# The first chunk of a four-layer hybrid network on one core: squares in four parts, weights in row buffers, two engines in written order

## The chip, the cores and the metric

One core of a Trainium2 chip runs the whole program in a single launch. The metric is the device time of one execution in microseconds (us). The program is a stack of four layers over 1040 tokens (16 learned tokens ahead of 1024), all in fp32, where each fp32 product is made of three products of "high" and "low" fp32r parts.

## What is computed

The reference, cut to what the change touches: the norm ahead of the first layer and that layer's projections. The other layers (a gated recurrence, a second recurrence, and attention again) follow in the same way.

```python
def rmsnorm(x, g):
    y = x * lax.rsqrt(jnp.mean(x * x, axis=-1, keepdims=True) + EPS)
    return y * g

def attention_branch(u, w_in, q_gain, k_gain, sinks, w_out, valid, pos):
    q, k, v, z = _split(u @ w_in, (A_W, A_KVW, A_KVW, A_W))
    q = rope(rmsnorm(q, q_gain), pos)
    k = rope(rmsnorm(k, k_gain), pos)
    o = sliding_window_attention(q, k, v, sinks, valid)
    return (o * silu(z)) @ w_out

for i in range(4):
    u = rmsnorm(h, norm_gain[i])
    h = h + branch[i % 3](u, ...)
```

## The kernel before

The residual `x` lies in SBUF as 8 tiles of 128 features by 1040 tokens. Tokens are worked in three chunks of 400, 384 and 256 (`CHUNKS`); a chunk's normalized input is kept as a high part `uh` and a low part `ul`, 8 tiles each, and the first 16 tokens again in `um`, 16 columns of high and 16 of low for each tile, so that the block of 16 tokens is one narrow operand.

The work is a list of steps, each with a cost, a function and perhaps a `pre` that loads and splits weights. TensorE (PE) runs in the order in which the steps are called. VectorE (DVE), ScalarE (ACT), GpSimd (POOL) and SyncE's transfers (SP) are ordered by the framework's scheduler from its own estimate of when each instruction can start. A `pre` is called ahead of its step by up to `LOOKAHEAD`.

The norm of a chunk: ACT squares the 8 tiles (`sq`, L369), DVE adds them (L373), PE multiplies the sum with a matrix of ones (`stat`, L381) so that each partition has the sum over all features, ACT makes the reciprocal root by Ln and Exp (`rstd_from`, L353 and L354), and then, for each tile, DVE multiplies x, gain and root (L407) and `split` copies the result rounded to fp32r on ACT (L187) and subtracts it on DVE (L188). For the first chunk POOL then copies 16 columns of either part to `um` (L412). Squares come in `PARTS` = 2 groups of four tiles, each with its own product with ones.

Weights come from HBM in halves of 512 columns: a transfer into one of two `raw` buffers (L232), then the same `split`. A key tile's first half holds feature tiles 0 to 3. The value weights are two pieces, `src0` with feature tiles 0 to 3 and `src1` with 4 to 7, in halves of two feature tiles.

The start: the 8 transfers of the first chunk of x, the norm's steps for chunk 0 (`norm.stats`, `norm.unit`), then the first layer's head. For chunk 0 that is `kv`: two of four parts of the key projection (feature tiles 0 to 3, L254), the value projection with the first four feature tiles for the four token blocks (L295 for the 16 tokens, L299 for three blocks of 128), the key's other two parts, and the value blocks' second halves. Into this the squares and products with ones of chunks 1 and 2 are put at shares `FIRST` of the head's cost. Then come chunk 1's key tile (a product of 384 columns), and so on.

## Time and profile before

| | |
|---|---|
| median of 3 runs | 2611.88 us |
| lowest and highest | 2609.99 and 2614.97 us |
| the profiled execution | 2610.83 us |
| its span, first to last instruction | 2609.0 us |
| mean granted TensorE clock | 0.995 |

Busy time is that of one engine summed over its instructions. PE's matmuls are pipelined, and their ends are modelled, so the distance from one start to the next says more than a duration does. An idle time stands in brackets behind an instruction with what ended it. "Granted clock" is the share of full speed that TensorE was allowed: 1.00 is 2.4 GHz and 0.50 is 1.2 GHz.

### The profile page before, as it was taken

What the parts mean: (1) busy time and instruction counts of PE and PEld (TensorE: products, weight loads), DVE (VectorE), ACT (ScalarE), POOL (GpSimd) and SP (SyncE); (2) the same over time, 40 slices, a digit from 0 to 9 for tenths busy, and PEclk for the clock granted to TensorE, in tenths of its full rate; (3) what the DMA queues carried; (4) which work ended last, traced back from release to release, by engine and by line L of the source; (5) the groups of instructions that cost most, each with busy time, mean ns of one, the idle gap of its engine ahead of it and who ended that gap; (6) DMA issues with size and microseconds to landing.
All of it is one profiled execution on the core that took longest, in us unless ns stands there. A gap on an engine that the chain in (4) does not pass through costs nothing.

```text
span 2609.0 us, 56062 instructions
## 1 busy us (share of the span) xinstructions
PE 2558.0 (98%) x21048; PEld 2459.0 (94%) x21048; DVE 1980.3 (76%) x5487; ACT 1725.9 (66%) x4757; POOL 154.1 (6%) x538
## 2 busy tenths in 40 slices
PE   7999999999999999999999999999999999999999
PEld 6899889899999999999999999999999999999999
DVE  6677777986767676767677788978787978677776
ACT  6777776566464646464646857878585867768872
POOL 1100100000000000000000000201001011000000
PEclk9999999999999999999999999999999999999999
DMA  4111111021111111111110101011110111111112
GB/s 136 56 43 50 46 37 47 17 67 58 41 58 41 58 41 58 41 58 41 55 61 34 57 27 42 30 38 34 34 42 26 42 62 45 54 44 47 53 38 82
DMA packets 74048, 126.81 MB, mean 49 GB/s; under 512 B 11552, under 2 KB 25760, under 8 KB 73776
## 3 DMA queue, kind: packets, MB, share of 16 engines
q1 hardware_dynamic: 73776, 123.23, 14.5%
q8 instruction: 165, 2.70, 0.4%
q14 instruction: 107, 0.88, 0.1%
HBM read 108.34 MB, written 4.26 MB: 43 GB/s over the span
## 4 chain that ended last, share of the span: by engine, by line
PE 81%; DVE 10%; ACT 6%; issue 1%; DMA 1%; POOL 0%; SPq 0%; DVEq 0%; ACTq 0%; POOLq 0%
PE pj L254 39%; PE pj L337 16%; PE pj L299 11%; PE po L682 2%; PE pt L660 1%; PE pm L614 1%; PE pm L615 1%; DVE t L407 1%; PE pa L534 1%; DVE ul L188 1%; PE po L918 1%; PE pj L295 1%; PE pm L890 1%; DVE X L1153 1%; DVE X L1155 1%
## 5 line engine op out<-in xcount | busy, mean ns | idle before, releaser
L254 PE MATMUL pj<-uh,wh 128*128 128x384 f32 (+2 forms) x2592 | 870.9, 336 | 3.7 <-ACT uh L187 3.6
L254 PE MATMUL pj<-ul,wh 128*128 128x384 f32 (+2 forms) x2592 | 835.3, 322 | 2.9 <-DVE ul L188 2.8
L254 PE MATMUL pj<-uh,wl 128*128 128x384 f32 (+2 forms) x2592 | 832.9, 321 | 0.1
L254 PEld LDWEIGHTS pj<-uh,wh 128*128 128x128 f32 x2592 | 491.3, 190 | 24.1 <-issue 12.7
L254 PEld LDWEIGHTS pj<-ul,wh 128*128 128x128 f32 x2592 | 491.2, 190 | 8.7 <-DVE ul L188 5.5
L254 PEld LDWEIGHTS pj<-uh,wl 128*128 128x128 f32 x2592 | 490.9, 189 | 0.5 <-DVE wl L188 0.4
L188 DVE TENSOR_TENSOR wl<-wr,wh 128x512 fp32r<-128x512 f32 x336 | 227.9, 687 | 58.1 <-ACT wh L187 55.4
L340 DVE TENSOR_TENSOR x<-x,pj 128x384 f32<-128x384 f32 (+2 forms) x480 | 235.4, 510 | 43.2 <-PE pj L337 41.3
L187 ACT CAST wh<-wr 128x512 fp32r<-128x512 f32 x337 | 203.3, 616 | 83.0 <-PE pj L337 26.8
L299 PE MATMUL pj<-wh,uh 128*128 128x256 f32 x896 | 258.1, 288 | 0.0
L337 PE MATMUL pj<-yh,wh 128*128 128x384 f32 (+2 forms) x768 | 253.0, 329 | 0.0
L299 PE MATMUL pj<-wh,ul 128*128 128x256 f32 x896 | 252.4, 282 | 0.0
L299 PE MATMUL pj<-wl,uh 128*128 128x256 f32 x896 | 252.3, 282 | 0.0
L337 PE MATMUL pj<-yl,wh 128*128 128x384 f32 (+2 forms) x768 | 247.4, 322 | 3.1 <-DVE yl L188 3.1
L337 PE MATMUL pj<-yh,wl 128*128 128x384 f32 (+2 forms) x768 | 246.8, 321 | 0.0
L299 PEld LDWEIGHTS pj<-wh,uh 128*128 128x128 f32 x896 | 169.3, 189 | 1.1 <-issue 0.3
L187 ACT CAST yh<-r 128x400 fp32r<-128x400 f32 (+2 forms) x144 | 68.6, 477 | 153.2 <-PE pj L337 141.7
L299 PEld LDWEIGHTS pj<-wl,uh 128*128 128x128 f32 x896 | 169.3, 189 | 0.5
L299 PEld LDWEIGHTS pj<-wh,ul 128*128 128x128 f32 x896 | 169.3, 189 | 0.0
L428 ACT ACTIVATE t<-t 128x384 f32<-128x384 f32 (+2 forms) x240 | 117.8, 491 | 76.5 <-DVE t L427 74.8
L427 DVE SCALAR_TENSOR_TENSOR t<-pj,t 128x384 f32<-128x384 f32 (+2 forms) x192 | 98.8, 514 | 78.2 <-ACT t L426 75.3
L337 PEld LDWEIGHTS pj<-yl,wh 128*128 128x128 f32 x768 | 144.9, 189 | 5.0 <-DVE yl L188 4.7
(265 smaller groups left out, 5431.4 us busy)
## 6 DMA issues: line engine op xcount, KB each, us to landing
wr<-in_b_win SPq DMA_DIRECT2D x128, 256.0 KB, 2.6
wr<-in_a_win SPq DMA_DIRECT2D x80, 256.0 KB, 2.7
wr<-in_c_win SPq DMA_DIRECT2D x64, 256.0 KB, 2.7
r<-rowsd SPq DMA_DIRECT2D x16, 520.0 KB, 5.4
wr<-in_a_wout SPq DMA_DIRECT2D x32, 256.0 KB, 2.7
wr<-in_b_wout SPq DMA_DIRECT2D x32, 256.0 KB, 2.6
t<-t SPq DMA_DIRECT2D x96, 48.0 KB, 1.9
wr<-in_c_wout SPq DMA_DIRECT2D x16, 256.0 KB, 2.7
```

The source lines that it names most:

```text
L187: s.copy(h, src)
L188: v.tensor_tensor(l, src, h.bitcast(F32), op=ALU.subtract)
L254: pe.matmul(acc[:, :cn], a[:, k, :], b[:, k, c0 : c0 + cn], start=(k == 0 and i == 0), stop=(k == KT - 1 and i == 2))
L295: pe.matmul(acc[:48, :256], um[:, k, :], m[:, kk, :], start=(k == 0 and m is wh), stop=(k == KT - 1 and m is wl))
L299: pe.matmul(acc[:cn, :256], a[:, k, c0 : c0 + cn], m[:, kk, :], start=(k == 0 and i == 0), stop=(k == KT - 1 and i == 2))
L337: pe.matmul(acc[:, :cn], a[:, k, mc], b, start=(k == 0 and i == 0), stop=(k == 1 and i == 2))
L340: v.tensor_tensor(x[:, m, c0 : c0 + cn], x[:, m, c0 : c0 + cn], acc[:, :cn], op=ALU.add)
L407: v.scalar_tensor_tensor(u, x[:, k, cs], ngain[:, self.i, k : k + 1], self.acc[n], op0=ALU.mult, op1=ALU.mult)
L427: v.scalar_tensor_tensor(a[:, :cn], z, 0.0, a[:, :cn], op0=ALU.min, op1=ALU.subtract)
L428: s.activation(a[:, :cn], a[:, :cn], AF.Exp)
L534: pe.matmul(st[:, 2 * k : 2 * k + 2], sq[:, z : z + P], R["masks"][:, 0:P:64], start=True, stop=True)
L682: pe.matmul(po[64 * hh : 64 * hh + 64, q0 - c0 : q0 - c0 + nq], V[kb][:kn, vc : vc + 64], ws[hh]["Pt"][:kn, u, ki, :nq], start=(ki == 0), ...
```

## The change

It concerns the first chunk of the first layer, and the order of what is loaded at the start.

- The first chunk's squares are taken in four parts of 4, 2, 1 and 1 tiles, so that four products with ones run in place of two. Chunks 1 and 2 keep two parts of four.
- The first key tile's weights and both pieces of the first value weights are loaded into three of the nine row buffers, straight behind x and the gains. Their splits are cut into halves (`late`) and placed by hand.
- From the first square to the last weight half of this stage, DVE and ACT run in program order. The written order is: the squares; the key's first half; Ln and Exp; then tiles 0 to 7, in which a tile's low part comes after the next tile's high part, with the key's second half behind tile 0, the value halves behind tiles 2, 3, 5 and 7.
- PE gets 12 products of zeros (`um`, 384 columns) ahead of the first product with ones, and 16 products of 128 columns behind the last.
- The 16-token copies become two for either half of the tiles, one on ACT and one on DVE, and no POOL copies. The memset of `um` moves from POOL to DVE.
- The value block of 16 tokens is multiplied after the three blocks of 128, in either half.
- The first layer's masks and columns are loaded ahead of the second chunk of x; the scaling of the columns and the two rope loads move to the end of the ordered stretch. `ident` is loaded later. Chunk 1's squares move to shares 0.4 to 0.95 of the head's cost from 0.3 to 0.9.

```diff
-PARTS = 2, 2, 2
-FIRST = 0.3, 0.9, 0.3, 0.7
+WARM = 12, 16
+FIRST = 0.4, 0.95, 0.3, 0.7
...
-    g.memset(um.bitcast(F32), 0.0)
+    v.memset(um.bitcast(F32), 0.0)
...
+    def load_row(src):
+        raw = row()
+        for z in (slice(0, 512), slice(512, 1024)):
+            sp.dma_start(raw[:, z], src[:, z])
+        return raw
+
     load_x(0)
-    sp.dma_start(ident, ins["ident"])
     sp.dma_start(ngain, ins["ngain"])
+    early = [load_row(ins["a_win"][0][k]) for k in (0, 2, 3)]
+
+    def warm(b, n):
+        def fn():
+            pe.matmul(psa()[:, : b.shape[-1]], rones, b, start=True, stop=True)
+
+        return [[0.0, fn, None] for _ in range(n)]
...
         for z in (slice(0, 512), slice(512, 1024)):
+            if row is not None:
+                late.append(lambda z=z: split(row[:, z], h[:, z], l[:, z]))
+                continue
...
+        def halves(self, n):
+
+            c0, cn = CHUNKS[n]
+            cs = slice(c0, c0 + cn)
+            u = {}
+
+            def high(k):
+                def fn():
+                    u[k] = tmp()[:, :cn]
+                    v.scalar_tensor_tensor(u[k], x[:, k, cs], ngain[:, self.i, k : k + 1], self.acc[n],
+                                           op0=ALU.mult, op1=ALU.mult)
+                    s.copy(uh[:, k, cs], u[k])
+
+                return [0.0, fn, None]
+
+            def low(k):
+                def fn():
+                    v.tensor_tensor(ul[:, k, cs], u[k], uh[:, k, cs].bitcast(F32), op=ALU.subtract)
+                    if k % 4 == 3:
+                        ks = slice(k - 3, k + 1)
+                        s.copy(um[:, ks, :NMETA], uh[:, ks, :NMETA].bitcast(F32))
+                        v.tensor_copy(um[:, ks, 32 : 32 + NMETA], ul[:, ks, :NMETA].bitcast(F32))
+
+                return [0.0, fn, None]
+
+            return [high(0)] + [z for k in range(1, KT) for z in (high(k), low(k - 1))] + [low(KT - 1)]
...
-            kv = kg0[0][:2] + vg[0][::2] + kg0[0][2:] + vg[0][1::2]
+            kp, vp = kg0[0], vg[0]
+
+            def take(step):
+                pre, step[2] = step[2], None
+
+                def first_half():
+                    pre()
+                    late.pop(0)()
+
+                return [0.0, first_half, None], [0.0, lambda: late.pop(0)(), None]
+
+            ordered = tc.manual_schedule(engines={mybir.EngineType.DVE, mybir.EngineType.Activation})
+            begin, end = [0.0, ordered.__enter__, None], [0.0, lambda: ordered.__exit__(None, None, None), None]
+            wk, wv0, wv1 = take(kp[0]), take(vp[0]), take(vp[1])
+            s0, u0 = first.stats(0, (4, 2, 1, 1)), first.halves(0)
+            kv = [begin] + warm(um.rearrange("p k c -> p (k c)"), WARM[0]) + s0[:-1] + [wk[0]] + s0[-1:]
+            kv += warm(rones, WARM[1]) + u0[:3] + [wk[1]] + u0[3:7] + [wv0[0]] + u0[7:9] + kp[:2]
+            kv += [wv0[1]] + u0[9:13] + [wv1[0]] + u0[13:] + [wv1[1], end]
+            kv += [vp[2], vp[4], vp[6], vp[0]] + kp[2:] + [vp[3], vp[5], vp[7], vp[1]]
...
-        head[0].insert(0, [0.0, enter, None])
+        if first:
+            enter()
+        else:
+            head[0].insert(0, [0.0, enter, None])
+        head[0].insert(head[0].index(end) if first else 1, [0.0, rope_load, None])
...
-    steps += norm.stats(0, PARTS[0]) + [norm.unit(0, k) for k in range(KT)]
...
-                st = norm.stats(n, PARTS[n])
+                st = norm.stats(n, (4, 4))
...
+    sp.dma_start(ident, ins["ident"])
     load_x(1)
```

## Rows read from the trace of the kernel before

**Rows 1.** Page, busy time of the engines over the span.

```profile
PE 2558.0 (98%) x21048; PEld 2459.0 (94%) x21048; DVE 1980.3 (76%) x5487; ACT 1725.9 (66%) x4757; POOL 154.1 (6%) x538
```

**Rows 2.** Stretches: us, busy per engine, granted clock, DMA share, GB/s.

```profile
5.00:10.00 5.00, 1.67 (x2) 0.50 (x2) 2.75 (x5) 3.62 (x7) 0.00 (x0) 1.00 0.99 324
...
0.00:50.00 50.00, 35.26 (x194) 29.39 (x195) 34.43 (x70) 33.37 (x70) 12.88 (x27) 0.97 0.52 165
...
100.00:150.00 50.00, 47.78 (x369) 43.10 (x370) 36.93 (x108) 39.15 (x133) 4.31 (x16) 1.00 0.14 40
...
900.00:950.00 50.00, 50.00 (x319) 49.83 (x318) 35.64 (x75) 25.72 (x58) 0.00 (x0) 1.00 0.13 43
```

**Rows 3.** Timeline (start, us, engine, line, operation, idle before): sums of squares.

```profile
6.51 2.68 ACT L369 ACTIVATE t<-x 128x400 f32<-128x400 f32 x5 [0.80 <-DMA x<-in_xT]
...
7.80 1.67 PE L381 MATMUL pa<-t,ones 128*128 128x400 f32 x2 [7.80 <-DVE t L373]
8.19 1.94 DVE L373 TENSOR_TENSOR t<-t,t 128x400 f32<-128x400 f32 x3 [0.54 <-ACT t L369]
...
10.18 1.70 PE L381 MATMUL pa<-t,ones 128*128 128x400 f32 x2 [0.71 <-DVE t L373]
...
11.92 0.59 ACT L353 ACTIVATE t<-pa,eps 128x400 f32<-128x400 f32 x1 [1.79 <-PE pa L381]
12.41 0.61 ACT L187 CAST wh<-wr 128x512 fp32r<-128x512 f32 x1
12.92 0.54 ACT L354 ACTIVATE t<-t 128x400 f32<-128x400 f32 x1
13.05 0.69 DVE L188 TENSOR_TENSOR wl<-wr,wh 128x512 fp32r<-128x512 f32 x1 [2.19 <-ACT wh L187]
13.66 1.72 DVE L407 SCALAR_TENSOR_TENSOR t<-x,ngain,t 128x400 f32<-128x400 f32 x3
```

**Rows 4.** Timeline: the normalized tiles of the first chunk.

```profile
14.32 1.61 ACT L187 CAST uh<-t 128x400 fp32r<-128x400 f32 x3 [0.87 <-DVE t L407]
...
15.30 1.54 DVE L188 TENSOR_TENSOR ul<-t,uh 128x400 fp32r<-128x400 f32 x3
...
18.88 1.28 DVE L188 TENSOR_TENSOR wl<-wr,wh 128x512 fp32r<-128x512 f32 x2
...
24.06 0.68 DVE L188 TENSOR_TENSOR wl<-wr,wh 128x512 fp32r<-128x512 f32 x1
```

**Rows 5.** Timeline, TensorE: products of the first chunk.

```profile
22.34 0.45 PE L295 MATMUL pj<-wh,um 128*48 128x256 f32 x1 [1.15 <-POOL um L412]
...
26.01 0.28 PE L299 MATMUL pj<-wh,ul 128*128 128x256 f32 x1
26.13 0.28 PE L299 MATMUL pj<-wh,uh 128*128 128x256 f32 x1
```

**Rows 6.** Stretches of half a us around the clock's fall and rise.

```profile
22.00:22.50 0.50, 0.16 (x1) 0.17 (x2) 0.46 (x2) 0.44 (x2) 0.50 (x3) 0.55 0.70 195
...
25.00:25.50 0.50, 0.50 (x4) 0.50 (x4) 0.40 (x2) 0.50 (x2) 0.26 (x1) 0.53 0.91 320
```

**Rows 7.** Timeline: end of the first chunk and the second chunk's norm.

```profile
32.04 0.81 PE L381 MATMUL pa<-t,ones 128*128 128x384 f32 x2
...
32.88 0.58 ACT L353 ACTIVATE t<-pa,eps 128x384 f32<-128x384 f32 x1 [0.21 <-PE pa L381]
...
34.05 1.68 DVE L407 SCALAR_TENSOR_TENSOR t<-x,ngain,t 128x384 f32<-128x384 f32 x3 [0.94 <-ACT t L354]
...
36.95 0.34 PE L254 MATMUL pj<-uh,wh 128*128 128x384 f32 x1
...
41.11 0.58 DVE L550 TENSOR_TENSOR r<-r,r 128x400 f32<-128x400 f32 x1
...
42.21 0.44 PE L254 MATMUL pj<-ul,wh 128*128 128x384 f32 x1 [0.44 <-DVE ul L188]
```

**Rows 8.** Timeline, SyncE: issue of the second chunk of x.

```profile
7.00 3.86 SPq L172 DMA_DIRECT2D x<-in_xT  x8
```

More of the change, by code (lines that the diff above doesn't have):

```diff
@@ L222, in gate_rows_proj, with weights @@
         return groups
-    def weights(src, kind, inrow=False):
+    late = []
+    def weights(src, kind, inrow=False, row=None):
         if inrow:
@@ L235, in weights, with proj @@
         return h.rearrange("p (k c) -> p k c", k=k), l.rearrange("p (k c) -> p k c", k=k)
-    def proj(src, evac, chunks=CHUNKS):
+    def proj(src, evac, chunks=CHUNKS, row=None):
         st = {}
         def pre():
-            st["w"] = weights(src, "m")
+            st["w"] = weights(src, "m", row=row)
         groups = []
@@ L269, in put_v, with proj_v @@
             s.copy(V[:cn, :256], acc[:cn, :256])
-    def proj_v(src0, src1, evac):
+    def proj_v(src0, src1, evac, rows=(None, None)):
         st = {}
         def pre0():
-            st[0] = weights(src0, "v")
+            st[0] = weights(src0, "v", row=rows[0])
         def pre1():
-            st[1] = weights(src1, "v")
+            st[1] = weights(src1, "v", row=rows[1])
         groups = []
@@ L365, in __init__, with sq @@
             self.i, self.acc, self.ps = i, {}, {}
-        def sq(self, m, n, c0, cn, size=KT):
+        def sq(self, m, n, c0, cn, new=None):
             q = tmp()[:, :cn]
             s.activation(q, x[:, m, c0 : c0 + cn], AF.Square)
-            if m % size == 0:
+            if m == 0 if new is None else new:
                 self.acc[n] = q
@@ L385, in stat, with stats @@
             return [4 * cn * MM, fn, None]
-        def stats(self, n, parts):
+        def stats(self, n, sizes):
             c0, cn = CHUNKS[n]
-            size = KT // parts
             def squares(part):
                 def fn():
-                    for m in range(part * size, (part + 1) * size):
-                        self.sq(m, n, c0, cn, size)
+                    m0 = sum(sizes[:part])
+                    for m in range(m0, m0 + sizes[part]):
+                        self.sq(m, n, c0, cn, m == m0)
                 return [0.0, fn, None]
-            return [z for k in range(parts) for z in (squares(k), self.stat(n, k, parts))]
+            return [z for k in range(len(sizes)) for z in (squares(k), self.stat(n, k, len(sizes)))]
+        def halves(self, n):
[18 more added lines that the diff above has]
+            return [high(0)] + [z for k in range(1, KT) for z in (high(k), low(k - 1))] + [low(KT - 1)]
         def unit(self, n, k):
@@ L450, in enter, with rope_load @@
             sp.dma_start(cons, ins["a_cols"][j])
+        def rope_load():
+            cons = R["cons"]
             v.tensor_scalar(cons[:, 0:1], cons[:, 0:1], 0.125, None, op0=ALU.mult)
@@ L512, in work_rows, with qk_proj @@
             return work
-        def qk_proj(src, gcol, work, fsplit, ch, scales=None):
+        def qk_proj(src, gcol, work, fsplit, ch, scales=None, row=None):
             late = {}
@@ L558, in finish @@
                         (D_Q[2], fsplit(lambda: late[n][0], n, c0, cn))]
-            return proj(src, evac, ch), [finish(n, *c) for n, c in enumerate(ch)]
+            return proj(src, evac, ch, row), [finish(n, *c) for n, c in enumerate(ch)]
         def tile_of(groups, events):
@@ L712, in layer_a @@
                           fin if t == 7 else None, t == 5) for t in (1, 3, 5, 7)}
-        kg0, kfin0 = qk_proj(win[0], 1, work_rows(3), k_split(0), CHUNKS)
+        kg0, kfin0 = qk_proj(win[0], 1, work_rows(3), k_split(0), CHUNKS, row=early[0] if first else None)
         kg1, kfin1 = qk_proj(win[1], 1, work_rows(1), k_split(1), CHUNKS)
-        vg = proj_v(win[2], win[3], v_evac)
+        vg = proj_v(win[2], win[3], v_evac, early[1:] if first else (None, None))
         qg = {t: qk_proj(win[4 + t], 0, tmps, q_split(t), chunks, t) for t in range(8)}
@@ L1342, in hybrid_kernel @@
         if i % 3 == 0:
-            head, body, oa, ob = layer_a(i, i // 3, tail is None, i == 3, fin)
+            head, body, oa, ob = layer_a(i, i // 3, norm if tail is None else None, i == 3, fin)
         elif i % 3 == 1:
@@ L1373, in hybrid_kernel @@
     ahead, k = 0.0, 0
-    while steps[k][2] is None:
-        k += 1
-    steps[k][2]()
-    steps[k][2] = None
+    sp.dma_start(ident, ins["ident"])
     load_x(1)
-    k = 0
     for n, (cost, fn, pre) in enumerate(steps):
```

## The prediction

> **What bounds the kernel now.** I read the busy times first, then stretches of 50 us, then the timeline of the first 45 us engine by engine, and last the granted clock in half-microsecond steps. TensorE is busy for 2558 of 2609 us [rows 1], and a stretch from the middle has no hole in it [rows 2]: there a change off TensorE gives nothing. Of the first 50 us TensorE is busy for 35.3 [rows 2], so 14.7 us are empty, and nearly all of them lie before 22.3. The change works on that hole alone.
>
> The hole goes like this. ScalarE's last square ends at 9.19 (6.51 + 2.68), VectorE's last addition at 10.13, and the second product with ones runs from 10.18 to the start of Ln at 11.92. Ln to the first normalizing instruction (call its start t, here 13.66) takes 1.74 us, since a weight cast at 12.41 stands ahead of Exp and a weight subtraction at 13.05 ahead of t [rows 3]. The second chunk has the same pair with nothing between: 32.88 to 34.05, 1.17 us [rows 7]. From t on VectorE is the limit: eight pairs of normalize and subtract, 0.57 and 0.51 us each, and four weight subtractions of 0.64, done by 24.74, which is t + 11.1 [rows 3, 4]. TensorE waits tile by tile, last 1.15 us for a GpSimd copy at 22.34; from there it runs without a break [rows 5] to the second chunk's first key product at 36.95, t + 23.3 [rows 7]. Two further gates follow: the second chunk's product with ones at 32.04, t + 18.4, and the tile that TensorE waits for at 42.21 [rows 7].
>
> **The change part by part.**
>
> *Squares in four parts.* The end no longer needs the last addition: 10.13 becomes 9.19, 0.94 us. But four products with ones replace two. One lasts 1.70 us at half clock [rows 3] and 0.81 at full [rows 7]; about 0.15 of either is drain and up to 0.2 is the first load, so in a chain each costs some 1.33 or 0.67 us. The second part's sum is there at about 8.75, since tiles 4 and 5 are squared by 8.13 and added in 0.58. All at full clock: 8.75 + 3 x 0.67 + 0.15 = 10.9 for Ln. All at half: 7.80 + 4 x 1.33 + 0.2 = 13.3. Two of each: 7.80 + 2.67 + 1.33 + 0.15 = 11.95 if the clock rises midway, 12.3 if it falls midway. Ln at 11.92 is what we have, so this part alone is worth between +1.0 and -1.4 us, near zero in the middle: TensorE has become the chain there, and the clock decides.
>
> *Weight halves around Ln and Exp.* The key's first half is cast right behind the last square (9.2 to 9.8 if landed by then), well before Ln, and the second half waits until behind tile 0. So 1.74 becomes 1.17: t = 12.1, 13.1 to 13.5, or 14.5. I take 13.3, a gain of 0.36.
>
> *Program order.* What comes behind t is longer. VectorE now has five weight halves there, not four, and each costs more than its 0.62: ScalarE casts it only after the tile's own cast, VectorE stands at the subtraction meanwhile, and ScalarE's next tile cast stands behind that. Walked through in units of rows 4 (normalize 0.57, hand-over to ScalarE 0.65 from start to start, tile cast 0.53, weight cast 0.61, subtract 0.50): key half 2 ends at t + 3.0, tile 3's low part at t + 7.5, the first value piece at t + 6.4 and 9.1, tile 7 at t + 14.2, the last weight half at t + 15.2. Of these 15.2 us, 12 are work and 3.3 are five waits of 0.6 to 0.8. Before, all this was over at t + 11.1. Queued behind each wait are the next tile's normalize and, for TensorE, its three products.
>
> *TensorE behind t.* The blocks of 128 tokens go first, so TensorE last waits at t + 9.1, for the value half with tiles 2 and 3. The GpSimd copies are gone and nothing of the 16 tokens is late: two pairs of copies of 64 columns, each under a 400-column cast (0.53 us) and at least nothing, stand on ScalarE and VectorE; I take 0.2 each, in the walk. What is left then is 66 products of 256 columns at 0.12, 16 narrow ones at 0.12, 12 of 400 columns at 0.18 and two products with ones at 0.65: 7.8 + 1.9 + 2.2 + 1.3 = 13.2 us, to t + 22.3 at full clock. Tile 7 (t + 14.2) and the last weight half (t + 15.2) are first used at t + 14.6 and t + 15.7, just in time. Now the clock: it stood at half from 22.0 to 25.4, after a stretch in which TensorE had waited tile by tile [rows 5, 6], and this cost 1.7 us. The new stretch up to t + 9.1 is as thin. With the same fall: t + 23.8. Before: t + 23.3.
>
> *Second chunk.* Its squares lie behind the ordered stretch: ScalarE is free at t + 14.5, eight squares take about 4 us, the last addition ends near t + 19.3; if the scheduler slips some into the waits, earlier. TensorE reaches the product at t + 18 (full) or t + 19.5 (half). So that gate comes at t + 18 to 19.5, against t + 18.4: +0.4 to -1.1.
>
> *What is hidden.* The 12 products of zeros (0.18 us each at full, twice that at half) end before the first product with ones at 7.80; if they didn't, the excess would be paid. The 16 small ones take 0.9 to 1.8 us of the 1.8 between the last product with ones and the first tile cast. The `um` memset stands on VectorE before any square is there. On SyncE's queue the second chunk of x, issued from 7.00 before [rows 8], now stands behind four more weight halves, the masks and the columns: some 1.3 MB, about 4 us at the 324 GB/s of 5 to 10 us [rows 2]; it then lands near 18 to 19, and its squares start at t + 14.5 = 27.8. Without that cover each us late would count. The third chunk and the rope rows move likewise; rope is read first at 41.11 [rows 7]. Whether casting from a row buffer costs other than from `raw` no row shows; the same shape on the same engine took 0.61 us [rows 3], and 0.1 us either way for six is the bound.
>
> *Sum.* Gain 0.36 at t; behind t, -0.5 at half clock or +1.0 at full, and by the second chunk -1.1 to +0.4: I take -0.1. Together 0.3 us off the profiled execution's 2610.83. On the median, 1.05 us higher, that is 2611.6. The corners are t = 12.1 with full clock, 2.2 us faster, and t = 14.5 with half, 2.0 us slower.
>
> One rule speaks for a better end. The Trainium skill (TensorE: Matmul & The Clock Gate, "What's actually happening") says that sustained work lifts the clock and that it falls back after an idle window. The trace has it falling at 22.05 although TensorE's last wait had been 1.15 us and it had done products shortly before [rows 5, 6]; by the row a thin stretch is enough. So I don't count on the zeros holding until 7.80.
>
> **The rivals.**
> 1. *Full clock throughout.* The zeros lift the clock and it stays: t = 12.1 and t + 22.3. Gain 2.1 us: 2609.8. For it: the skill's rule above. Against: some two us without a product between the zeros (begun at about 1.3, 4 us at half clock) and 7.80, and the fall at 22.05.
> 2. *The written order doesn't hold VectorE.* If weight casts slip ahead of tile casts, the 3.3 us of waits go and TensorE's last wait is near t + 6.5: 2.6 us more, 2609.0, with rival 1 as well 2607.2. Against: the order is written, cast behind cast.
> 3. *Slower: half clock through the four products.* t = 14.5, end t + 23.8, the second chunk's squares late: 2613.6. It decides if the clock is at half at 7.80 and doesn't rise before the fourth product; the two products before were at half (1.70 us).
> 4. *The rest is ordered anew.* Everything later is ordered by the scheduler from estimates that now start elsewhere. From 100 to 150 TensorE stands idle for 2.2 us [rows 2], and each fall of the clock costs 1.7. Two or three such pieces either way: 2607 or 2616.
>
> **How the numbers follow.** No change to speak of 0.54, rival 1 0.14, rival 2 0.10, rival 3 0.12, rival 4 0.10 (0.06 for faster). About 0.2%, 5.2 us, is what a measurement of this kernel can tell from no change. The corners of the sum lie within it; beyond it on the fast side are half of rival 2 and most of rival 4's fast half, and a tail of rival 1, 0.13; on the slow side rival 4's slow half and a tail of rival 3, 0.07; the rest is 0.80. The range holds all but the outer parts of rival 4 and of rival 2, with the scatter of the runs of before (2610.0 to 2615.0): 2606.5 to 2615.0.
>
> **What the new profile would show.** Right: Ln between 11 and 13 with no weight cast between it and Exp; VectorE idle 0.6 to 0.8 us ahead of each weight subtraction behind t, released by ScalarE; no GpSimd copy; last low part at about t + 14; the first 384-column key product between 34.5 and 38. Wrong if: the four products with ones follow at 0.67 us (rival 1); VectorE has no such waits (rival 2); Ln comes after 13 (rival 3); or the start gains and loses as told, and the time still moves by over 3 us, in stretches behind 50 (rival 4).

## The result: 0.23% slower

| | before | after |
|---|---|---|
| median of 10 runs each, side by side | 2610.55 us | 2617.07 us |
| lowest and highest | 2607.12 and 2614.97 | 2611.86 and 2620.13 |
| ratio, with 95% interval | | 1.0023 (1.0014 to 1.0033) |
| the profiled execution, and its span | 2610.83 and 2609.0 us | 2620.13 and 2618.3 us |
| mean granted clock of that execution | 0.995 | 0.993 |

The time lies 5.5 us above the forecast and 2.1 us above the upper end of its range. The profiled execution is the slowest of the ten, so 3 us of its 9.3 us are scatter. Another profile of the changed kernel (run e5 below) spans 2615.2 us, and another of the kernel before (e6) 2608.3.

Busy times (the page) and stretches of the changed kernel (as [rows 1] and [rows 2]):

```profile
PE 2569.9 (98%) x21080; PEld 2469.2 (94%) x21080; DVE 1979.7 (76%) x5488; ACT 1725.4 (66%) x4759; POOL 143.5 (5%) x521
```

```profile
0.00:50.00 50.00, 41.03 (x204) 34.11 (x204) 31.67 (x67) 31.04 (x66) 2.32 (x10) 0.93 0.50 164
50.00:100.00 50.00, 45.68 (x315) 41.94 (x315) 34.20 (x90) 38.28 (x110) 2.05 (x9) 0.97 0.20 61
100.00:150.00 50.00, 47.78 (x356) 43.18 (x355) 34.83 (x100) 36.37 (x123) 5.09 (x17) 0.97 0.14 40
900.00:950.00 50.00, 50.00 (x306) 50.00 (x305) 33.17 (x68) 29.74 (x69) 0.00 (x0) 1.00 0.13 43
```

TensorE is 5.8 us busier in the first 50 us. Its added products more than account for that: the zeros take 4.18 us, and four products with ones take 5.67 where two took 3.37. VectorE does 2.8 us less there: it falls behind.

The timeline of the changed kernel up to t, the first normalizing instruction (as [rows 3]; start, us, engine, line, operation, count, idle before; each fp32 product counts as two instructions):

```profile
1.45 4.18 PE L186 MATMUL pa<-um,ones 128*128 128x384 f32 x12 [1.45 <-DVE um L167]
7.51 5.67 PE L398 MATMUL pa<-t,ones 128*128 128x400 f32 x8 [1.88 <-DVE t L390]
...
5.53 3.27 ACT L386 ACTIVATE t<-x 128x400 f32<-128x400 f32 x6 [1.39 <-DMA x<-in_xT]
8.93 0.62 ACT L199 CAST wh<-r 128x512 fp32r<-128x512 f32 x1
13.22 0.59 ACT L370 ACTIVATE t<-pa,eps 128x400 f32<-128x400 f32 x1 [3.67 <-PE pa L398]
13.84 0.54 ACT L371 ACTIVATE t<-t 128x400 f32<-128x400 f32 x1
...
14.41 1.18 DVE L427 SCALAR_TENSOR_TENSOR t<-x,ngain,t 128x400 f32<-128x400 f32 x2 [4.14 <-PE pa L186]
```

The last square ends at 8.80, earlier than the 9.19 of before, but Ln waits until 13.22 for four products that stand back to back from 7.51: 5.67 us, 1.4 each.

VectorE and TensorE from t on (as [rows 4, 5, 7]):

```profile
16.70 0.69 DVE L200 TENSOR_TENSOR wl<-r,wh 128x512 fp32r<-128x512 f32 x1 [0.49 <-ACT wh L199]
...
20.08 0.69 DVE L200 TENSOR_TENSOR wl<-r,wh 128x512 fp32r<-128x512 f32 x1 [0.62 <-ACT wh L199]
...
22.58 0.69 DVE L200 TENSOR_TENSOR wl<-r,wh 128x512 fp32r<-128x512 f32 x1 [0.54 <-ACT wh L199]
...
25.96 0.69 DVE L200 TENSOR_TENSOR wl<-r,wh 128x512 fp32r<-128x512 f32 x1 [0.62 <-ACT wh L199]
...
28.07 0.57 DVE L435 TENSOR_TENSOR ul<-t,uh 128x400 fp32r<-128x400 f32 x1
28.55 0.55 DVE L390 TENSOR_TENSOR t<-t,t 128x384 f32<-128x384 f32 x1
29.02 0.19 DVE L439 CAST um<-ul 128x64 fp32r<-128x64 f32 x1
29.12 0.69 DVE L200 TENSOR_TENSOR wl<-r,wh 128x512 fp32r<-128x512 f32 x1
...
29.86 2.35 DVE L390 TENSOR_TENSOR t<-t,t 128x384 f32<-128x384 f32 x4
```

```profile
21.86 0.70 PE L271 MATMUL pj<-ul,wh 128*128 128x400 f32 x1 [1.53 <-DVE ul L435]
...
30.56 0.88 PE L398 MATMUL pa<-t,ones 128*128 128x384 f32 x2 [0.49 <-DVE t L390]
...
34.90 0.81 PE L398 MATMUL pa<-t,ones 128*128 128x384 f32 x2
...
39.32 0.33 PE L271 MATMUL pj<-uh,wh 128*128 128x384 f32 x1
```

The written order's waits are there, and tile 7's low part comes at 28.07, t + 13.66. The last addition to the second chunk's first sum of squares starts at 29.86, behind that part and the last weight half. At 30.56 TensorE stands for VectorE at the *first* of the second chunk's two products with ones, which reads this sum; 8.76 us of its work lie between that product and the second chunk's first key product.

One table for all profiles, the experiments' too, in us from t, but for t itself. "Ln" is counted from the end of the last square; "low 7" is tile 7's low part; "ones 1, 2" are the second chunk's products with ones; "key" is its first key product.

```
                           t      Ln   low 7  ones 1  ones 2   key
before                   13.66   2.73   9.91   14.60   18.38   23.29
before, again (e6)       12.86   2.67   9.90   13.47   17.34   22.25
after                    14.41   4.42  13.66   16.15   20.49   24.91
after, again (e5)        13.21   2.97  13.66   16.15   20.49   24.91
e1  no products          14.08   4.14  13.66   16.07   20.43   24.84
e3  two parts            12.85   2.71  13.67   16.16   21.91   25.15
e4  own order            13.87   2.84  10.26   13.31   19.19   23.61
e7  22 of zeros          12.36   1.90  13.66   16.15   20.49   24.91
e8  e1 + e3 + e4         13.33   2.72   9.67   12.62   18.40   21.64
e9  first ones later     13.27   3.40  13.66   17.14   20.05   24.57
e10 no small products    14.23   4.28  13.66   16.15   20.47   24.89
e11 22, none, later      11.95   1.86  13.66   17.97   20.88   25.41
e12 e8, shares of before 13.20   2.70   9.67   12.63   19.51   23.93
e13 before, four parts   14.19   4.32   9.17   14.88   18.66   23.56
e14 e11, own order       12.33   1.93  10.28   15.44   17.51   21.93
e16 e8, first later      13.54   2.71   9.68   12.90   14.97   19.38
e17 e16, written order   12.82   2.70  13.66   16.79   19.70   24.23
e18 e16 again            13.30   2.70   9.68   13.05   15.11   19.53
e2  before, 32 small     12.98   2.54   9.90   13.20   16.98   21.89
e15 before, 38 small     13.89   3.17   9.84   14.74   18.52   23.42
```

### The profile page after: what moved, and what is told of

The parts are those of the page before. It is cut to its first block, busy times and chain, and to the rows that moved or that the text cites. A ratio compares the mean times of both kernels' runs of the same rounds, so it can differ in the third digit from the quotient of the medians.

```text
span 2618.3 us, 56111 instructions
## 1 busy us (share of the span) xinstructions
PE 2569.9 (98%) x21080; PEld 2469.2 (94%) x21080; DVE 1979.7 (76%) x5488; ACT 1725.4 (66%) x4759; POOL 143.5 (5%) x521
## 3 DMA queue, kind: packets, MB, share of 16 engines
q8 instruction: 166, 2.72, 0.4%
## 4 chain that ended last, share of the span: by engine, by line
PE 80%; DVE 11%; ACT 6%; issue 2%; DMA 1%; SPq 0%; POOL 0%; DVEq 0%; ACTq 0%; POOLq 0%
PE pj L271 38%; PE pj L354 16%; PE pj L316 11%; PE po L729 2%; PE pt L707 1%; PE pm L661 1%; PE pa L581 1%; PE pm L662 1%; DVE t L451 1%; DVE ul L200 1%; PE po L987 1%; PE pm L959 1%; ACT Sm L686 1%; PE pj L312 1%; DVE wl L200 1%
```

## The experiments

Each run's time is a median of 11, and its ratio, with a 95% interval, is to 21 to 33 runs of the kernel before, timed beside it. The intervals are some 0.0009 wide to either side, 2.3 us, so two runs that differ by less than about 3 us are not told apart by their times alone. Diffs are against the changed kernel unless another is named.

**The two kernels once more.** e5 is the changed kernel, e6 the kernel before (a profile and a single time, 2610.1 us).

> The changed kernel itself, profiled and timed once more, to tell what of its first trace is the change and what is that one execution. Theory E (the loss is in the first chunk and carried, the rest is where each execution's half-clock stretches happen to fall): first 384-column key product again 1.5 to 4 us later than the 34.9 to 37.0 of the kernel before, but the difference between 75 and 300 us does not repeat: other stretches at half clock than 95.5 and 116 us. Theory A (weight halves land late at fixed places): the same two late landings near 91 and 218 us. Time 2615 to 2618 us either way.

> The kernel before itself, profiled once more. Theory E: its first 384-column key product moves between 34.5 and 37.5 us with the place of the half-clock stretch, and the stretches behind 50 us fall elsewhere than 80, 261 and 517 us. Theory A: the same places. One time, 2605 to 2616 us.

e5: 2616.51 us, 1.0023 (1.0014 to 1.0032). The loss is there again, and so are the two late weight halves: 4.6 us after issue at 85.24 and 4.2 after issue at 211.53.

**e1, no products of zeros and no small ones; e7, more of zeros.**

```diff
-WARM = 12, 16
+WARM = 0, 0      # e1;  e7: 22, 16
```

> The changed kernel without its 28 products of zeros and ones ahead. Theory A (the start costs 2.4 to 2.8 us, by TensorE's half clock through four products with ones and by VectorE's waits; the rest of the loss comes later in layer one, because 64 more TensorE instructions shift the points at which TensorE's next block of instructions is fetched, and the fetch then shares a transfer engine with a weight half that is needed at once): t (first normalizing instruction) stays near 14.4, since the four products were at half clock with the zeros too; the later loss of 3 to 4 us goes; 2613 to 2614 us against 2610.6 for the kernel before and 2617 for the changed one. Rival B (the zeros help the start and the loss is all in the start or its order): t later by 0.5 us or more, total 2617 to 2618.

> The changed kernel with 22 products of zeros in place of 12, so that TensorE is not idle for two us before the first product with ones at 7.5. Theory E: with 12 the clock is back at half by then or during the four products (they ran 0.67 us per load in the changed kernel, half clock); with 22 it is up from about 6 us and stays, the four products take 0.7 us each or less, Ln at 11 to 11.5 instead of 13.2, t at 12.2 to 12.7 instead of 14.4, the first 384-column key product 1.5 to 2 us earlier: 2615. Rival F (zeros do nothing for the clock): t at 14 or later, 2617 or more.

e1: 2614.9 us, 1.0018 (1.0009 to 1.0026). e7: 2613.92 us, 1.0019 (1.0010 to 1.0028). Without any such products t is 14.08 and Ln comes 4.14 us behind the last square. The five traces with 12 of zeros and four parts have 2.84 to 4.42 there, so the 12 helped in some executions and not in others. With 22 they reach up to the products with ones:

```profile
1.45 6.20 PE L186 MATMUL pa<-um,ones 128*128 128x384 f32 x22 [1.45 <-DVE um L167]
7.50 0.83 PE L398 MATMUL pa<-t,ones 128*128 128x400 f32 x2
8.84 2.28 PE L398 MATMUL pa<-t,ones 128*128 128x400 f32 x6 [0.51 <-DVE t L390]
```

The clock is up (0.83 us a product), Ln comes 1.90 us behind the last square and t at 12.36. That is the prediction's full-clock rival, and yet the second chunk's key product stands at t + 24.91 as in the changed kernel: from t to there the clock isn't what binds.

**e3, two parts; e13, four parts in the kernel before.**

```diff
-            s0, u0 = first.stats(0, (4, 2, 1, 1)), first.halves(0)
+            s0, u0 = first.stats(0, (4, 4)), first.halves(0)
```

```diff
# e13, against the kernel before, with stats() and sq() taking sizes as in the changed kernel
-PARTS = 2, 2, 2
+PARTS = (4, 2, 1, 1), (4, 4), (4, 4)
```

> The changed kernel with the first chunk's squares in two parts of four again. Theory A: the last addition ends near 9.5 and one product with ones of 1.7 us at half clock follows, Ln at 11.3 instead of 13.2, t at 12.5 instead of 14.4, first 384-column key product 1.5 to 2 us earlier than 39.3; the loss behind 50 us stays: 2615 to 2615.5. Rival C (four parts are no burden): t not before 14, 2617.

> The kernel before with one part of the change: the first chunk's squares summed in four parts (4, 2, 1, 1). Theory A (the products with ones follow at 0.67 us, as in the changed kernel, and the four are the chain): Ln comes 1 to 1.3 us later against the last square than in the kernel before (there 2.7 us behind its end), t moves by that, and the time is 2611 to 2612, not to be told from the kernel before. Rival (the prediction's step: one addition less on the chain): Ln comes up to 1 us earlier against the last square and the time is 2609.5 to 2610.5.

e3: 2614.02 us, 1.0014 (1.0005 to 1.0023). e13: 2611.71 us, 1.0005 (0.9996 to 1.0014). The four parts alone, in the kernel before (TensorE, then ScalarE):

```profile
7.29 5.67 PE L381 MATMUL pa<-t,ones 128*128 128x400 f32 x8 [7.29 <-DVE t L373]
...
13.00 0.59 ACT L353 ACTIVATE t<-pa,eps 128x400 f32<-128x400 f32 x1 [2.14 <-PE pa L381]
```

The column "Ln" of the table gives their price: 2.7 us behind the last square with two parts; with four, 4.1 to 4.4 where all of it runs at half clock, 2.8 to 3.4 where the clock changes midway, 1.9 at full clock. Theory A of e13 holds for Ln. The total of e13 doesn't show it. In e3, against its expectation, a second loss is gone as well, far behind the start (see e10 below), so its time doesn't price the four parts.

**e4, VectorE and ScalarE in the scheduler's order; e8, that with two parts and no products.**

```diff
-            ordered = tc.manual_schedule(engines={mybir.EngineType.DVE, mybir.EngineType.Activation})
+            ordered = ExitStack()
```

> The changed kernel with VectorE and ScalarE ordered by the scheduler as before, the steps called in the same sequence. Theory A: weight casts are put into ScalarE's idle time, VectorE's waits of 0.6 us ahead of weight subtractions go in part, the last low part ends 1 to 3 us earlier than 28.6 after t; TensorE's first 384-column key product 0 to 2 us earlier than 39.3: 2615 to 2617. Rival D (the written order is no burden): tile 7 and the key product as in the changed kernel or later, 2617 or more.

> The changed kernel with squares in two parts of four, VectorE and ScalarE in the scheduler's order, and no products ahead: what stays are the row buffers for weights, the 16-token copies in two, the blocks of 128 first and the order of loads. Theory E (the loss lies in four parts at half clock and in the written order): t at 12 to 13, the first 384-column key product at 35 to 37, time 2609.5 to 2611.5, no slower than the kernel before. Rival G (the loss lies in what stays, as the second chunk of x landing later): 2613 or more.

e4: 2613.52 us, 1.0012 (1.0003 to 1.0021). e8: 2612.59 us, 1.0010 (1.0001 to 1.0019). The scheduler's order brings tile 7's low part to t + 10.3 and t + 9.7. TensorE now reaches the second chunk's first product with ones earlier, and waits 2.09 us there in e4 and 1.26 in e8. e4 came out faster than its expectation (2615 to 2617), e8 slower than theory E's, though it evacuates the third chunk's first key tile at 57.53, between the two traces of the kernel before (57.93 and 56.11).

**e9, the second chunk's first product with ones later; e11, that with 22 of zeros and no small ones; e12, e8 with the shares of before.** Of e9 and e11 the first product stands twelve key products later, the second where it was.

```diff
-FIRST = 0.4, 0.95, 0.3, 0.7
+FIRST = 0.6, 0.90, 0.3, 0.7      # e9 and e11; e12: 0.3, 0.9, 0.3, 0.7
-WARM = 12, 16
+WARM = 22, 0                     # e11; e12: 0, 0
```

> The changed kernel with the second chunk's first product with ones placed twelve 400-column key products later on TensorE; its second product stays where it was. Theory A (TensorE, in program order, loses time at that first product, which it reaches before VectorE, held by the written order, has made the sum, t + 16.15): it now has 2.2 us of products in front, so its idle time of 0.5 to 1.4 us goes, and the first key product of the second chunk comes at t + 23.4 to 24.4 instead of t + 24.9; the kernel is some 1 us faster, 2615 to 2616. Rival (the second product, or the tiles of the second chunk, gate the start anyway): the first key product moves, but the evacuation of the third chunk's key stays at t + 46.3, and the time at 2616.5.

> The changed kernel with 22 products of zeros, without the 16 small ones, and with the second chunk's first product with ones twelve key products later. If the three losses found so far add up (half clock in the products with ones 1.3 us at t; the wait at the second chunk's first product about 1 us; late weight halves 1 to 2 us), t is at 12.4, the second chunk's first key product at t + 23.4 to 24.4, and the time is 2612 to 2613.5. If the second chunk is gated elsewhere, t is at 12.4 and the time that of the run with 22 products of zeros alone, 2614.

> The changed kernel with two parts, no products of zeros or small products, VectorE and ScalarE in the scheduler's order, and the second chunk's products with ones placed as in the kernel before (0.3, 0.9). What is left of the change is the weights in row buffers, the copies of 16 tokens in pairs, and the order of blocks and loads. The run with 0.4, 0.95 had its second product with ones at t + 18.4 and lost 1.6 us between the second chunk's first key product and the third chunk's evacuation. If that placing was its loss: the evacuation comes at t + 43.5 to 44.5 (t + 45.9 there) and the time is 2610 to 2611, that of the kernel before. If the rest of the change costs by itself: 2612.5 again.

e9: 2616.22 us, 1.0021 (1.0012 to 1.0030). e11: 2613.03 us, 1.0009 (1.0000 to 1.0018). e12: 2612.84 us, 1.0008 (1.0000 to 1.0017). In e9 the first product no longer waits, and the second one does (TensorE, then VectorE):

```profile
30.41 0.81 PE L398 MATMUL pa<-t,ones 128*128 128x384 f32 x2
33.32 0.91 PE L398 MATMUL pa<-t,ones 128*128 128x384 f32 x2 [0.67 <-DVE t L390]
...
32.04 1.22 DVE L390 TENSOR_TENSOR t<-t,t 128x384 f32<-128x384 f32 x2 [2.29 <-ACT t L386]
```

The key product moves by 0.35 us. The rival holds: one gate was taken away and the next stood right behind it. e11's time is the one expected if three losses add up, but its key product isn't: it comes at t + 25.41 in place of 23.4 to 24.4, since the second product waits 0.69 us for VectorE there too. In e12 the first product is reached too early, and TensorE waits longer than the change of shares was to give back:

```profile
25.83 1.02 PE L398 MATMUL pa<-t,ones 128*128 128x384 f32 x2 [1.92 <-DVE t L390]
```

**e14, e11 in the scheduler's order; e16, e8 with the first product later; e17, e16 in the written order; e18, e16 once more.** These separate the order from everything else: e11 and e14 differ by it alone, and so do e17 and e18, which ran side by side.

```diff
# e16 and e18; e17 has the manual_schedule line again
-WARM = 12, 16
-FIRST = 0.4, 0.95, 0.3, 0.7
+WARM = 0, 0
+FIRST = 0.55, 0.85, 0.3, 0.7
...
+            ordered = ExitStack()
+            s0, u0 = first.stats(0, (4, 4)), first.halves(0)
```

> The changed kernel with 22 products of zeros, no small ones, the second chunk's first product with ones twelve key products later, and VectorE and ScalarE in the scheduler's order. Theory A (the written order holds VectorE by some 4 us from t to tile 7's low part, and through it both of the second chunk's products with ones): tile 7's low part comes at t + 9.5 to 10.5 (t + 13.7 with the written order), TensorE doesn't wait for either product, the second chunk's first key product comes at t + 21.5 to 23, and the time is 2610 to 2611.5, not to be told from the kernel before. Rival (the waits come from elsewhere, such as the second chunk of x landing late): the waits of 0.5 to 2 us at those products stay and the time is that of the same kernel in the written order, 2613.

> The changed kernel with two parts, no products of zeros or small products, the scheduler's order, and the second chunk's first product with ones twelve key products later than in the run before of this kind (where TensorE stood 1.9 us at it). Theory A (that wait was what the rest of the change still lost): no wait there, the second chunk's first key product at t + 21.5 to 23 (t + 23.9 there), the time 2610.5 to 2611.5. Rival (weights in row buffers and the new order of loads cost by themselves behind the start): 2612.5 to 2613.

> The run e16 (two parts, no products of zeros or small ones, the second chunk's first product with ones twelve key products later) with VectorE and ScalarE in the written order again, and nothing else. Theory A (the written order makes VectorE wait behind every weight cast): tile 7's low part at t + 13 to 14 instead of t + 9.7, the second chunk's second product with ones waits for VectorE, its first key product comes at t + 23.5 to 25 instead of t + 19.4, and the time is 2612 to 2614. Rival (the order is harmless once the products with ones are placed later): key product at t + 19.4 to 21, time 2607 to 2609.

> The run e16 once more, unchanged. If its lead is real: the second chunk's first key product at t + 19 to 21, 2606 to 2609 us, 0.05 to 0.15% under the kernel before. If it was the luck of one call: 2610 to 2611.

e14: 2609.34 us, 0.9997 (0.9988 to 1.0006). e16: 2607.11 us, 0.9992 (0.9984 to 1.0001). e17: 2613.14 us, 1.0012 (1.0003 to 1.0021). e18: 2610.96 us, 1.0001 (0.9992 to 1.0010). The stretch 12 to 24 us of e17 and then of e18 (busy time of PE, PEld, DVE, ACT, POOL, clock, DMA share, GB/s):

```profile
12.00:24.00 12.00, 8.11 (x28) 6.51 (x29) 9.17 (x17) 6.32 (x14) 0.00 (x0) 1.00 0.99 328
```

```profile
12.00:24.00 12.00, 9.14 (x55) 8.70 (x56) 11.31 (x25) 9.11 (x21) 0.24 (x1) 1.00 0.98 321
```

Nothing but the order has changed, and VectorE does 11.31 us of work in place of 9.17, ScalarE 9.11 in place of 6.32. (The clock's 1.00 is no reading here: its first record comes at 23.6 in e17 and at 18.4 in e18, and ahead of it the products run at half pace. That is not the cause: tile 7's low part comes at t + 13.66 in e7 too, where the clock was up at t.) e17's second product with ones waits for VectorE, e18's waits for nothing (TensorE, e17 and then e18):

```profile
29.61 0.81 PE L398 MATMUL pa<-t,ones 128*128 128x384 f32 x2
32.52 0.91 PE L398 MATMUL pa<-t,ones 128*128 128x384 f32 x2 [0.69 <-DVE t L390]
```

```profile
26.35 0.81 PE L398 MATMUL pa<-t,ones 128*128 128x384 f32 x2
28.41 0.81 PE L398 MATMUL pa<-t,ones 128*128 128x384 f32 x2
```

The key product comes at t + 24.2 in the written order and t + 19.5 in the other. The median differs by 2.2 us between e17 and e18, the ratio by 0.0012 (3 us) between e11 and e14 and by 0.0011 between the changed kernel and e4. Each of these is near the edge of what the intervals tell, but all three point one way, and the traces show the mechanism. Theory A holds. e16 was faster than expected (2610.5 to 2611.5), but its lead over the kernel before did not hold when it was timed again: 0.9992 and then 1.0001, so no kernel here is shown to beat it.

**e2 and e15, more TensorE instructions in the kernel before; e10, the changed kernel without its 16 small products.** They ask about the part of the loss behind the start. TensorE's instructions are themselves transferred during the run, on a DMA queue of their own (q8), and a weight half can be on its way at the same time.

```diff
# e2 and e15, against the kernel before
     load_x(0)
+    for _ in range(32):      # e15: 38
+        pe.matmul(psa()[:, :8], rones, rones[:, :8], start=True, stop=True)
# e10, against the changed kernel
-WARM = 12, 16
+WARM = 12, 0
```

> The kernel before with 32 products of 8 columns at its very start, while TensorE waits for x, and nothing else: 64 TensorE instructions more, as in the changed kernel. Theory A: t as before (13.7), first key product of 384 columns as before (37.0), then weight halves that land in 4 to 5 us instead of 2.7 near 86 and 210 us, and 3 to 4 us lost: 2613.5 to 2615. Rival B: no difference, 2610.6.

> The changed kernel without its 16 small products; the 12 of zeros stay. This takes 32 instructions off TensorE ahead of everything else, so its instruction fetches come some 2.3 us later in the work than in the changed kernel, behind the landing of the weight half issued near 86 us and 2 us further from the issue of that near 214. Theory B (a fetch that starts 0.9 to 2.2 us after a weight half is issued can make it land near 4.5 us after issue instead of 2.8, and TensorE waits for it): those two land after less than 3.2 us, the start stays as it was (first key product of the second chunk at t + 24.9), and the time falls by 1 to 2 us to 2615. Rival (the late landings are covered, or come from something else): they stay, or go without moving the time from 2616.5.

> The kernel before with 38 products of 8 columns ahead of the first product with ones, on an idle TensorE. With 32 of them a fetch of TensorE's instructions started 2.1 us behind the issue of the weight half near 81 us and it landed in 2.9 us; six more bring the fetch some 0.9 us nearer. Theory B (a fetch 0.9 to 2.2 us behind the issue makes it land near 4.5 us): that half lands after 4 us or more, TensorE waits for it by 1 to 2 us, and the time is 2611 to 2612. Rival: it lands in under 3.2 us, or lands late without moving the time from 2610.

e2: 2609.85 us, 0.9999 (0.9989 to 1.0009). e10: 2614.64 us, 1.0016 (1.0007 to 1.0025). e15: 2610.7 us, 1.0003 (0.9994 to 1.0012). First what the changed kernel shows (SyncE's issue of two weight halves, ScalarE's cast of the first, TensorE's next wait; below them the DMA view of 86.3 to 91.1):

```profile
86.34 1.02 SPq L249 DMA_DIRECT2D wr<-in_a_win  x2
...
91.07 0.62 ACT L199 CAST wh<-wr 128x512 fp32r<-128x512 f32 x1 [2.24 <-DMA wr<-in_a_win]
...
94.24 0.62 PE L707 MATMUL pt<-ident,Sm 128*128 128x128 f32 x2 [3.50 <-ACT Sm L690]
```

```profile
q8 instruction: 1, 0.02, 1.3%
issues: line engine op xcount, KB each, median us to landing
wr<-in_a_win SPq DMA_DIRECT2D x2, 256.0 KB, 4.7
```

The same place in e10, where TensorE has 32 instructions fewer ahead of it and no instruction transfer falls between issue and landing:

```profile
86.30 0.98 SPq L249 DMA_DIRECT2D wr<-in_a_win  x2
...
89.28 0.62 ACT L199 CAST wh<-wr 128x512 fp32r<-128x512 f32 x1 [0.56 <-DMA wr<-in_a_win]
...
92.46 0.62 PE L707 MATMUL pt<-ident,Sm 128*128 128x128 f32 x2 [1.81 <-ACT Sm L690]
```

```profile
wr<-in_a_win SPq DMA_DIRECT2D x2, 256.0 KB, 3.0
```

The half lands 4.7 us after issue there and 3.0 here, and TensorE waits 1.7 us less. The half issued at 214.5 of the changed kernel does the same (its cast waits 3.01 us):

```profile
218.86 0.62 ACT L199 CAST wh<-wr 128x512 fp32r<-128x512 f32 x1 [3.01 <-DMA wr<-in_a_win]
```

e10 keeps the start (key at t + 24.89) and is 1.9 us under e5 and 1.6 under e9, which ran beside it. That is theory B's forecast, though a difference of this size is not clear of the noise by itself. How much of it a trace places: from the first addition to x (185.53 in the changed kernel) to the 144th (825.51) pass 640.0 us, in e5 640.2, in e9 640.5. All three have a half there that lands 4.2 to 4.3 us after issue. In both traces of the kernel before it is 636.5 and 636.1, in e1 636.5 and in e10 637.6. Over all 20 traces the long stretch goes with the number of TensorE's instructions. The five with 21080 matmuls (after, e5, e9, e4 in the scheduler's order, and e2, which is the kernel before with 32 more) take 639.6 to 640.7 us; the fifteen with another number take 636.1 to 637.6, e3 with its 21076 among them (636.4). So neither the written order nor the four parts make this loss.

e15 misses its expectation: the half near 83 landed in 3.1 us, since the fetch came 2.55 us behind the issue and not 1.2, and the time stayed. So it tests nothing of that place. e2 misses its expectation too (2613.5 to 2615). It has a half issued at 206.6 that landed after 4.5 us, and 639.6 us for the stretch just named, yet its median is that of the kernel before. So e2's profile has this loss of some 3 us, and its median doesn't show it.

## Why the prediction failed

*What bounds the kernel: half right.* The change touched the hole before 22.3 us, as told. "The change works on that hole alone" is the first step that failed: the sum has no term for what lies behind, and more than half of the loss in the traces is there. Up to the first addition to x the mean of the two traces of after is 184.0 us, that of before 179.2: 4.8 us, of which 3.1 are there by the third chunk's first key tile. From the first addition to the 144th it loses 3.8 more, and behind it nothing (1792.6 us against 1793.1 to the end of the span). These traces are 8.0 us apart in the mean, the medians 6.5. In the 3.8 us there are two pieces. In the trace of after TensorE waits 1.15 us at 220.91, behind the late weight half, and is some 1.5 us later from there on. Then the clock falls at 269.6 and stays at half for 6.8 us, against 3.4 or none near there in all traces but after, e5 and e9. The prediction's own price is 1.7 us for 3.4 us at half.

```profile
220.91 1.09 PE L729 MATMUL po<-Pt,v 128*64 128x128 f32 x14 [1.15 <-DVE Pt L710]
```

```profile
272.00:276.00 4.00, 4.00 (x25) 3.45 (x24) 2.34 (x9) 2.09 (x7) 0.00 (x0) 0.50 0.18 51
```

*Squares in four parts: the right sum, the wrong value taken.* "All at half: 13.3" for Ln is what came: 13.22. The four followed at 1.4 us each; the text had 1.33. It then took the middle, 12 or so, for t = 13.3, and said "TensorE has become the chain there, and the clock decides". It did: the clock stayed low until 13.6 in the trace of after, and rose at 10.8 in e5, with t at 14.41 and 13.21 (these rises are the clock's first records; ahead of them the products' spacing tells its level, though the column of the granted clock says 1.00). The 12 products of zeros did not settle it: Ln comes 2.84 to 4.42 us behind the last square with them, 4.14 in e1 without.

*Weight halves around Ln and Exp: right.* Ln to t took 1.19 us, against 1.17 told.

*Program order: right.* Five waits were told, of 0.6 to 0.8 us each; four of them measure 0.49 to 0.62, and the fifth was covered. Tile 7's low part starts at t + 13.7 and ends at t + 14.2 (t + 14.2 told). The Trainium skill (PSUM — Partial Sum Buffer, "Engine vs sequencer instructions") calls the queues of VectorE and ScalarE strictly first in, first out; by the rows the trace agrees, since 0.5 to 0.6 us of VectorE stand idle ahead of each such half with a ready tile queued behind it.

*TensorE behind t and the second chunk: the second step that failed.* The text followed TensorE to t + 22.3 at full clock or t + 23.8 at half (24.0 by its own price of 1.7 us for the fall), and let one product with ones gate it, the second, at "t + 18 to 19.5". There are two, and the first stands earlier in TensorE's queue. TensorE's last wait for a tile came at t + 7.45, not at t + 9.1, so it was early at that first product. Its sum of squares is finished on VectorE behind tile 7's low part, and the product starts at t + 16.15, the same in after, e5, e7 and e10 whatever the clock did; 8.76 us of TensorE's work follow, and t + 24.9 comes out. The text wrote that the squares "lie behind the ordered stretch" and applied it to the second product alone. e9 then showed that the second one was gated too (0.67 us of wait). And the clock's fall lasted twice as long as told: it stood at half from 20.4 to 27.3, against 3.4 us before [rows 6]. The text overlooked that before t and up to 18.6 the kernel before had run at half too (its first record), so that from t on it had the longer time at half. Two stretches in and at the end of the fall:

```profile
20.50:21.00 0.50, 0.00 (x0) 0.00 (x0) 0.50 (x2) 0.00 (x0) 0.00 (x0) 0.50 0.91 284
27.00:27.50 0.50, 0.50 (x5) 0.50 (x5) 0.50 (x2) 0.27 (x1) 0.00 (x0) 0.75 0.00 0
```

With 22 products of zeros (e7) it stood at half from 16.4 to 23.2, in e1 from 16.4 to 26.6, and the key product stayed at t + 24.8 to 24.9. So the clock was no term of this part of the sum; the written order was. Against the mean of the two traces of before (t + 22.8) the key product is 2.1 us late. Instead of the 0.3 us gained, the third chunk's first key tile was evacuated at 60.70 and 59.49 (after, e5), against 57.93 and 56.11: 3.1 us late.

*What is hidden: right at the start, wrong behind it.* The zeros ended at 5.63, ahead of 7.51. The second chunk of x was there when its first square began at 25.83. Casting from a row buffer took 0.62 us. e16 and e18 keep the row buffers and the new order of loads, and lose nothing by them. But hidden products are instructions too: with the 16 small ones gone (e10) the weight halves near 86 and 214 landed in time, and the median fell by 1.9 us.

*Rivals.* Rival 1 (full clock) gave its t in e7 (12.36 for 12.1) and not its time. The sum's fast corner, 2.2 us, doesn't come out of its own terms: 1.56 us at t and 1.0 by the products make 2.6, or 0.4 by the gate 2.0. Rival 2 did not come. Rival 3 gave the right t for the trace of after, 14.41 for 14.5, while its 2613.6 leaves out what the order cost behind t and what was lost behind 50 us. Rival 4 named the place behind 50 us and a price, 2616, that is nearly the result. Longer falls of the clock, which it counted in, are part of the loss. But its cause was wrong: from some 50 us on, VectorE, ScalarE, GpSimd and SyncE run the same operations in the same order in both kernels. What moved is where TensorE's instruction transfers fall among the weight transfers.

*What stays open.* That the number of TensorE's instructions and a late weight half cost the changed kernel some 2 us rests on the stretch above and on e10, e1, e3 and e7, which have other numbers and medians 1.6 to 2.6 us under e5, the last three with changes at the start as well. In the kernel before it was not shown in time: e2 has the long stretch in its trace and not in its median, and e15 missed. From the third chunk's first key tile to the first addition to x the traces scatter between 120.2 and 126.4 us, and what orders them is the clock. The three without half clock there (e1, e3, e9) take 120.2 to 120.8 us, the twelve with 3.4 us of it 121.7 to 123.1, the three with 6.8 us (after, e10, e11) 123.2 to 124.8, the two with 10.2 us (e4, e17) 126.4 and 125.5. The changed kernel is 1.7 us longer there, and this explains about half of it: its two traces have 6.8 and 3.4 us at half, the kernel before 3.4 in both. Why the clock falls more often or for longer in one trace than in another is not shown.

## What to carry to other kernels

Where one engine's order is written by hand, list every instruction of the *next* stage that an in-order consumer meets before the end of this one, the first of them above all, and see when its producer gets to it behind the written stretch: the waits written into VectorE here (0.5 to 0.6 us each) were paid by TensorE behind the end of the stretch, at 30.56. A gate that is taken away is worth only the distance to the next one (e9: 0.35 us), so price the two together. And an edit at the start can move things far behind it that nobody reordered: for effects of a few us, compare stretches of the trace between fixed pieces of work, and the time at half clock in each, before believing a sum that ends where the edit ends.

## What the runs showed of the hardware

*Weight loads land late when one of TensorE's instruction transfers starts about 1 us behind their issue.* Queue q8 moves 16 KB at a time (2.72 MB in 166 transfers) in the changed kernel, one for each 254 of TensorE's 42160 instructions (matmuls and weight loads); that they are TensorE's is inferred from this count and from e10. Over 20 traces of these kernels, weight halves of 256 KB issued behind 60 us, by the distance from their issue to the nearest start of such a transfer:

```
transfer starts, us behind the issue    halves   median us to landing   over 3.4 us
-3 to -0.75                                525            2.7                2%
-0.75 to 0.75                              339            3.1               19%
0.75 to 1.75                               182            3.8               86%
1.75 to 2.25                               153            2.7               19%
2.25 to 6                                  969            2.7                2%
none from -3 to 6                         2151            2.7                2%
```

That the one causes the other is an inference from this distance and from e10, where moving the transfer took the delay away.

*The clock fell again behind products of zeros.* 12 of them at 1.45 to 5.63 did not keep the clock up for products at 7.51: in e3 and e4, which have them too, it had risen at 6.0 and 4.4 us and was at half again from 9.4 and 7.9. The Trainium skill (TensorE: Matmul & The Clock Gate, "What's actually happening") has the clock rise with sustained work and fall after an idle window; by these rows and e7's the trace agrees, though in after, e5 and e10 the same 12 products brought no rise before 10.8. What a clock kept up gave for the four products was 2.2 to 2.5 us of Ln (1.9 in place of 4.1 to 4.4).
